# A hybrid decoder step on one core: one buffer for inner features after the first step, and four reordered pieces of side work

## The chip, the core and the metric

The kernel runs on one core of a Trainium2 chip. Its time is the device time of one execution in microseconds, given as the median of the runs. TensorE (PE) does the matmuls, VectorE (DVE), ScalarE (ACT) and GpSimd (POOL) do the elementwise work, and SyncE (SP) issues the transfers. Each engine works off its own queue in program order: an instruction that waits holds up all that stand behind it on its engine.

## What is computed

One layer of inference on 1024 prompt tokens and 8 x 8 decode tokens (1088 in all), width 1024, in float32. The output is compared with this reference, cut here to what matters:

```python
h = rmsnorm(x, g_mix_pre) * (1 + scale_m) + shift_m
sc_b, sc_c, sc_x, z, xbc, dt = split(h @ w_in)
y_sc = sc_b * causal_dwconv(sc_c * sc_x, sc_conv_w)        # also returns the new conv state
y_ssd = ssd_scan(silu(causal_dwconv(xbc)), dt, ...)        # 16 heads, 4 groups
y_ssd = rmsnorm((y_ssd * silu(z)) per group) * ssm_norm_g  # four norms, one for each group
x = x + gate_m * rmsnorm(concat(y_sc, y_ssd) @ w_out, g_mix_post)
h2 = rmsnorm(x, g_ffn_pre) * (1 + scale_f) + shift_f
x = x + gate_f * rmsnorm((silu(h2 @ w_gate) * (h2 @ w_up)) @ w_down, g_ffn_post)
```

## The kernel before, in words

Every float32 operand of a large matmul is split into two parts, hi (a cast, done by ScalarE, line 1039 or 311) and lo (the difference, done by VectorE, line 1040 or 312), and each product is three matmuls: hi by hi, hi by lo, lo by hi. So a weight tile that arrives by DMA costs a cast on ScalarE and a subtraction on VectorE before PE can use it, and the third matmul of a chain needs the lo part. The function `part` does one such split.

From the short-convolution columns on, and in the FFN, blocks are multiplied with seven products instead of eight (`unit`). Products are taken in the order 1, 5, 6, 3, 7, 2, 4; the sums of weight blocks that some of them need are made by `combos_w`, those of the features by `sums_h`, `sums_last` and `sums_x`. `plain_w` splits four weight blocks without sums.

The stretches that matter here, in order of time:

1. The gates z of groups 2 and 3 (`gate_late`), with the steps of the generator `sums` in between. Group 3's weights are split by `plain_w`, called at line 1186, behind gate 2.
2. Four pairs of column tiles of the short convolution. Each pair runs three units, cc, cx and cb (`sc_unit`), then the convolution. Beside the units of the first pair the norms of groups 2 and 3 (`norm`) are taken in steps: sums of squares, an rsqrt chain of small VectorE operations on a tile sm, a broadcast on PE (line 291), multiplications (line 939), the split into hi and lo (lines 298 and 299) and the store of both halves to y_d in DRAM (`y_out`). The tiles y of pair 1 take the memory of group 3's.
3. The output projection in phases. The first takes the SSD half, eight column tiles in four pairs mp, and calls `conv_state`, which transposes the new conv state (8 transposes, 2 copies, 2 stores). Then `out_proj` adds the other half for three ranges of tokens, and runs a generator `tail` (`mix_tail`) of the tokens whose sum is complete: transposes and squares of the first four column tiles; the same of the last four, then rsqrt, residual (line 1260) and its squares; a second rsqrt and a scaling; transposes back.
4. The FFN. `plain_step(j, q)` does block j of the inner width for token half q with plain products: four gate blocks (evacuated by ScalarE into sg), four up blocks (multiplied by VectorE into f), and `inner_out`, which writes f and sums of it into f_d in DRAM through tiles fs. Those come in turn from the pools in the list `st_from`. Steps (0,0) and (1,0) come first, while `tail` generators finish the tokens of the second half; then the memory `tailp` is closed, a new pool `xc1a` is laid out where it was, `plain_x` makes x__1224 to x__1227 in it, and step (0,1) begins with them.

What sets the order: the program is written in one order, a scheduler with priorities puts it into engine queues, and work that is wrapped in `in_order` or `chained` may not pass the last PE instruction before it. Pools of memory add waits: a tile waits for the last reader of what its memory held before. The list `st_from` at the FFN's start:

```python
    st_from.append(pool(tailp, "stx", 1))
    plain_step(0, 0, ...)
    ...
    plain_step(1, 0, ...)
    run(tail_a, tail_b)
    st_from.pop(st_from.index(next(p for p in st_from if p is not st0)))
    tailp.close()
```

Of the kernel before, what the change touches and what calls it, by code (L numbers as in the profile page):

```python
# [33 lines left out]
def hymba_step(ctx, tc, i, o):  # L34
# [927 lines left out]
    def run(*gens):  # L962
        for gen in gens:
            for _ in gen:
                pass
# [100 lines left out]
    def plain_w(w, cols, raws=None):  # L1066
        raws = raws or [raw_half(w, j, cols) for j in range(2)]
        W = {}
        for m in range(2):
            for j in range(2):  # L1070
                t = in_turn(w_from).tile([P, 2, 4, P], F32R, tag="wc", name=nm("wp_"))
                part(t[:, 0], t[:, 1], raws[j][:, :, m * P:(m + 1) * P])
                W[m, j] = [[t[:, s, k] for k in range(4)] for s in range(2)]
        return W

# [105 lines left out]
        return psy.tile([P, 2, 384], F32, tag="sq", name=nm("sq"))  # L1181

    sums = sums_h()
    norm2, norm3 = (norm(g, ys[g], sq_row, sx_row) for g in (2, 3))
    gate_late(2, ys[2], [[v[:, k] for v in w for k in range(KT)] for w in w_next], {n: [sums] for n in range(6)})
    W = plain_w(w_in, 3072 + 768, raw_next[:2])
    gate_late(3, ys[3], [[W[m, j][s][k] for s in range(2) for j in range(2) for k in range(4)] for m in range(2)],
              {n: [sums] for n in range(6)})
    run(sums)
# [3 lines left out]
    def sc_unit(cols, tiles, between):  # L1193
        unit(combos_w(w_in, cols, nc.vector), X_sc, 4, [0, 1],
             lambda q, i, h: tiles[i][:, SQ[q][0] + 272 * h:SQ[q][0] + 272 * (h + 1)], True, between, SQ, chained)

    kept = []
    for pr in range(4):
        cc, cx = [yt((pap, yp2)[pr % 2]) for _ in range(2)], [yt(yp4) for _ in range(2)]
        sc_unit(1024 + 256 * pr, cc, {})  # L1200
        sc_unit(2048 + 256 * pr, cx, {n: [norm2, norm2] for n in range(7)} if pr == 0 else {})
        if pr == 0:
            run(norm2)
        if pr == 2:
            conv_state(ncs, 16, 3, o["ssmc_p"], o["ssmc_s"])
        ext = []
        for m in range(2):
            ct = 2 * pr + m
            e = yt(yp4, (P, YT))
            es = e[:, 2 + NP:2 + NP + 80].rearrange("p (b t) -> p b t", b=8)  # L1210
            nc.vector.tensor_tensor(e[:, 2:2 + NP], cc[m][:, :NP], cx[m][:, :NP], op=mult)
            nc.vector.tensor_tensor(es[:, :, 2:10], bt(cc[m][:, NP:]), bt(cx[m][:, NP:]), op=mult)
            keep_tail(e, es, hscT[:, ct, :], nsc[:, ct, :], 2)
            conv(cc[m], e, es, [scw[:, j, ct:ct + 1] for j in range(3)], ct, None)
            ext.append(e)
        cb = [yt(yp4) for _ in range(2)]
        sc_unit(256 * pr, cb, {n: [norm3, norm3] for n in range(7)} if pr == 0 else {})
        if pr == 0:
            run(norm3)
        for m in range(2):  # L1220
            y, hi, lo = cc[m], ext[m][:, :T].bitcast(F32R), cb[m].bitcast(F32R)
            nc.vector.tensor_tensor(y, y, cb[m], op=mult)
            split(hi, lo, y)
            kept.append((2 * pr + m, hi, lo))
        if pr < 3:
            while kept:
                y_out(*kept.pop(0))
# [62 lines left out]
    for mp in range(4):  # L1290
        for m, (wh, wl) in enumerate(load_cols(w_out, mp * 256, 2, D)):
            for c0, n in OC:
                ps = pm()
                acc3(ps, n, [(wh[:, k, :], wl[:, k, :], first[k][0][:, c0:c0 + n], first[k][1][:, c0:c0 + n])
                             for k in range(KT)])
                nc.scalar.copy(acc_at(2 * mp + m, c0, n), ps[:, :n])
        if mp == 0:
            while kept:
                y_out(*kept.pop(0))
        if mp == 2:  # L1300
            conv_state(nsc, 8, 2, o["scc_p"], o["scc_s"])


    def out_split(c):
# [22 lines left out]
    def out_proj(c, terms, steps_, load, pairs=range(4)):  # L1327

        for mp in pairs:
            for m, w in enumerate(load(mp)):  # L1330
                m += 2 * mp
                in_order(out_tile, c, terms, w, m)
                for gen in steps_.get(m, ()):
                    in_order(next, gen, None)
# [52 lines left out]
    nxt = next_splits()  # L1387
    out_proj(0, terms[0], {0: [nxt], 2: [nxt]}, out_load)
    tail = mix_tail([0, 1, 2, 3], lambda t: load_x(t, fb, "fm"), rows_fm, G_m)
    out_proj(1, terms[1], {0: [tail], 1: [tail], 4: [tail]}, out_load)  # L1390
    out_proj(2, terms[2], {1: [tail], 2: [tail]}, out_load, (0, 1))


# [64 lines left out]
    def mark():  # L1458
        while True:
            marks.append(in_line())  # L1460
            yield
# [117 lines left out]
    tail_b = mix_tail([6, 7, 8], x_tl, row_tl, G2)  # L1579
    st_from.append(pool(tailp, "stx", 1))  # L1580
    plain_step(0, 0, ({0: [tail_b], 2: [tail_b], 3: [tail_a]}, {0: [tail_a], 1: [tail_a, mark()], 3: [tail_b]}))
    raw_from = [btp] * 4
    w_from = [slots[1]] * 4 + [slots[0]] * 4
    g0 = sums_x([xc0], 0)
    s0 = behind(g0)
    plain_step(1, 0, ({0: [tail_b], 1: [tail_b]}, {1: [s0], 2: [s0], 3: [s0]}))
    run(tail_a, tail_b)
    st_from.pop(st_from.index(next(p for p in st_from if p is not st0)))
    tailp.close()
    xc1 = [pool(left, "xc1a", 1)]  # L1590
    run(plain_x(xc1[0], 1))
# [176 lines left out]
```

## Time and profile before

| | |
|---|---|
| median of 3 runs | 1768.85 us (1767.85 to 1770.19) |
| profiled execution | 1771.54 us, its span 1769.8 us |
| mean granted clock of PE | 0.983 |
| PE busy | 1695.9 us, 96% of the span |
| DVE busy | 1170.4 us, 66% |
| ACT busy | 777.2 us, 44% |
| POOL busy | 210.8 us, 12% |

A share of the span is an average over stages. PE's queue is what ends last nearly everywhere, so the table is read together with PE's own waits: where PE stands idle, the timeline names the instruction that released it. [...]

### The profile page before, as it was taken

Reading aid. Unit: us, or ns where it says so; the run is one execution under the profiler, and the core shown is the slowest. Engines: PE = TensorE matmul, PEld = TensorE weight load, DVE = VectorE, ACT = ScalarE, POOL = GpSimd, SP = SyncE. Lnnn points to the kernel's source line nnn. Section 1 sums busy time; section 2 is a strip of 40 time slices with the busy share of each in tenths; the row PEclk is TensorE's granted clock in tenths of the full one; section 3 lists DMA queues with packets and bytes.
Section 4 is the critical chain, followed back from the end, with each engine's and each line's share of the span. In section 5 each row is a group of like instructions: output and inputs, shape, how many; then the busy total and the mean of one; then the engine's idle time right before and its main releaser. Section 6 shows DMA issues by size and latency. Waiting matters only on the chain.

```text
span 1769.8 us, 31580 instructions
## 1 busy us (share of the span) xinstructions
PE 1695.9 (96%) x12628; PEld 1608.7 (91%) x12628; DVE 1170.4 (66%) x2264; ACT 777.2 (44%) x1601; POOL 210.8 (12%) x317
## 2 busy tenths in 40 slices
PE   5999999999999999999999979999999999899997
PEld 4898888898899999998989979999999999899987
DVE  5578677777888676551137769666665676677845
ACT  3447454557444333322227755444444454422303
POOL 2110000000000000000000000122222200322303
PEclk9999999999999999999999989999999999999999
DMA  9201345442222422258275542334344349756243
GB/s 317 69 18 32 112 148 158 139 124 76 102 72 99 149 87 65 99 207 278 74 242 190 181 155 88 114 137 164 139 149 149 137 146 336 299 213 237 99 152 120
DMA packets 160634, 259.74 MB, mean 147 GB/s; under 512 B 10561, under 2 KB 124401, under 8 KB 158182
## 3 DMA queue, kind: packets, MB, share of 16 engines
q1 hardware_dynamic: 160486, 257.71, 42.8%
q8 instruction: 99, 1.62, 0.4%
q14 instruction: 49, 0.40, 0.1%
HBM read 186.30 MB, written 71.38 MB: 146 GB/s over the span
## 4 chain that ended last, share of the span: by engine, by line
PE 81%; DVE 8%; ACT 4%; DMA 3%; issue 2%; POOL 1%; SPq 1%; DVEq 0%; ACTq 0%; POOLq 0%
PE pm L334 10%; PE pm L336 10%; PE pm L335 9%; PE pz L1078 7%; PE pz L1080 7%; PE pz L1079 7%; PE pm L1080 6%; PE pm L1078 6%; PE pm L1079 6%; DMA raw<-in_w_in 1%; PE pm L209 1%; PE pz L751 1%; PE pz L756 1%; PE pz L745 1%; PE pz L723 1%
## 5 line engine op out<-in xcount | busy, mean ns | idle before, releaser
L312 DVE TENSOR_TENSOR wl<-raw,wh 128x512 fp32r<-128x512 f32 (+1 forms) x87 | 61.4, 730 | 99.9 <-ACT wh L311 99.2
L334 PE MATMUL pm<-h,wh 128*128 128x384 f32 (+1 forms) x342 | 114.8, 336 | 0.0
L335 PE MATMUL pm<-h,wh 128*128 128x384 f32 (+1 forms) x342 | 114.5, 335 | 0.0
L336 PE MATMUL pm<-h,wl 128*128 128x384 f32 (+1 forms) x342 | 113.7, 334 | 0.0
L336 PE MATMUL pm<-hb,wl 128*128 128x512 f32 (+2 forms) x320 | 107.5, 337 | 1.9 <-DVE wl L312 1.9
L335 PE MATMUL pm<-hb,wh 128*128 128x512 f32 (+2 forms) x320 | 107.4, 337 | 0.0
L334 PE MATMUL pm<-hb,wh 128*128 128x512 f32 (+2 forms) x320 | 105.4, 336 | 1.3 <-ACT wh L311 1.3
L311 ACT CAST wh<-raw 128x512 fp32r<-128x512 f32 (+1 forms) x89 | 56.4, 664 | 113.5 <-PE pm L335 70.0
L1040 DVE TENSOR_TENSOR fs<-f,fs 128x576 fp32r<-128x576 f32 (+2 forms) x80 | 56.0, 713 | 28.2 <-ACT fs L1039 27.3
L1039 ACT CAST fs<-f 128x576 fp32r<-128x576 f32 (+2 forms) x80 | 46.6, 597 | 51.3 <-DMA f_d<-fs 22.1
L336 PEld LDWEIGHTS pm<-hb,wl 128*128 128x128 f32 x320 | 60.7, 190 | 7.4 <-DVE wl L312 2.1
L1095 DVE TENSOR_TENSOR facc<-facc,pz 128x288 f32<-128x288 f32 x124 | 55.9, 451 | 16.9 <-PE pz L1080 16.5
L334 PEld LDWEIGHTS pm<-hb,wh 128*128 128x128 f32 x320 | 60.5, 190 | 7.1 <-ACT wh L311 1.6
L334 PEld LDWEIGHTS pm<-h,wh 128*128 128x128 f32 x342 | 65.2, 191 | 1.6 <-issue 0.9
L335 PEld LDWEIGHTS pm<-h,wh 128*128 128x128 f32 x342 | 65.2, 191 | 1.4 <-issue 0.7
L336 PEld LDWEIGHTS pm<-h,wl 128*128 128x128 f32 x342 | 64.9, 190 | 1.3 <-issue 1.0
L335 PEld LDWEIGHTS pm<-hb,wh 128*128 128x128 f32 x320 | 60.7, 190 | 5.1
L1095 DVE TENSOR_TENSOR facc<-facc,pm 128x256 f32<-128x256 f32 x124 | 51.5, 415 | 6.5 <-PE pm L1080 5.6
L334 PE MATMUL pm<-bt,wh 128*128 128x384 f32 (+2 forms) x146 | 51.6, 353 | 0.0
L336 PE MATMUL pm<-bt,wl 128*128 128x384 f32 (+1 forms) x146 | 48.5, 332 | 0.2 <-DVE wl L312 0.2
L1057 POOL TENSOR_TENSOR raw<-raw 128x512 f32<-128x512 f32 x16 | 22.6, 1412 | 217.0 <-DVE raw L1055 208.4
L335 PE MATMUL pm<-bt,wh 128*128 128x384 f32 (+2 forms) x146 | 47.7, 327 | 0.0
(7510 smaller groups left out, 6390.0 us busy)
## 6 DMA issues: line engine op xcount, KB each, us to landing
raw<-in_w_in SPq DMA_DIRECT2D x48, 512.0 KB
fc<-f_d SPq DMA_DIRECT2D x9, 2016.0 KB
f_d<-fs SPq DMA_DIRECT2D x31, 576.0 KB
wa<-in_w_ada SPq DMA_DIRECT2D x32, 512.0 KB
raw<-in_w_out SPq DMA_DIRECT2D x32, 512.0 KB
fc<-f_d SPq DMA_DIRECT2D x9, 1792.0 KB
f_d<-fs SPq DMA_DIRECT2D x31, 512.0 KB
raw<-in_w_gate SPq DMA_DIRECT2D x28, 512.0 KB
```

The source lines that it names most:

```text
L311: (nc.gpsimd.tensor_copy if hi_eng else nc.scalar.copy)(wh, raw)
L312: (eng or nc.vector).tensor_tensor(wl, raw, wh, op=sub)
L334: mm(ps[:, :n], wh, xh, start=(first and j == 0), stop=False)
L335: mm(ps[:, :n], wh, xl, start=False, stop=False)
L336: mm(ps[:, :n], wl, xh, start=False, stop=(last and j == end))
L1039: nc.scalar.copy(hi, v)
L1040: (eng or nc.vector).tensor_tensor(lo, v, hi, op=sub)
L1057: eng.tensor_tensor(a21, a11, a21, op=sub)
L1078: mm(ps, W[0][k], X[0][k], start=(start and k == 0), stop=False, skip_group_check=True)
L1079: mm(ps, W[0][k], X[1][k], start=False, stop=False, skip_group_check=True)
L1080: mm(ps, W[1][k], X[0][k], start=False, stop=(stop and k == nk - 1), skip_group_check=True)
L1095: nc.vector.tensor_tensor(out(q, i, h), out(q, i, h), ps, op=add)
```

## The change

Five edits, none of which adds or removes an instruction on any engine:

- the split of gate 3's weights is written ahead of gate 2;
- the norms of groups 2 and 3 become one generator `norms`, stepped once in the last four products of cc, once in each product of cx and twice in each of cb, without the calls that ran them to their ends;
- `conv_state` for the short convolution runs in order, behind the third pair of the first phase;
- the steps of `tail` in the second phase stand behind column tiles 0, 2 and 5 instead of 0, 1 and 4;
- after step (0,0), `st_from` holds st0 alone, so that step (1,0) writes all its fs tiles through one buffer and none through stx, which lies in `tailp`.

```diff
--- before.py
+++ after.py
@@ -1181,9 +1181,9 @@
         return psy.tile([P, 2, 384], F32, tag="sq", name=nm("sq"))
 
     sums = sums_h()
-    norm2, norm3 = (norm(g, ys[g], sq_row, sx_row) for g in (2, 3))
+    norms = itertools.chain(*(norm(g, ys[g], sq_row, sx_row) for g in (2, 3)))
+    W = plain_w(w_in, 3072 + 768, raw_next[:2])
     gate_late(2, ys[2], [[v[:, k] for v in w for k in range(KT)] for w in w_next], {n: [sums] for n in range(6)})
-    W = plain_w(w_in, 3072 + 768, raw_next[:2])
     gate_late(3, ys[3], [[W[m, j][s][k] for s in range(2) for j in range(2) for k in range(4)] for m in range(2)],
               {n: [sums] for n in range(6)})
     run(sums)
@@ -1197,10 +1197,8 @@
     kept = []
     for pr in range(4):
         cc, cx = [yt((pap, yp2)[pr % 2]) for _ in range(2)], [yt(yp4) for _ in range(2)]
-        sc_unit(1024 + 256 * pr, cc, {})
-        sc_unit(2048 + 256 * pr, cx, {n: [norm2, norm2] for n in range(7)} if pr == 0 else {})
-        if pr == 0:
-            run(norm2)
+        sc_unit(1024 + 256 * pr, cc, {n: [norms] for n in range(3, 7)})
+        sc_unit(2048 + 256 * pr, cx, {n: [norms] for n in range(7)})
         if pr == 2:
             conv_state(ncs, 16, 3, o["ssmc_p"], o["ssmc_s"])
         ext = []
@@ -1214,9 +1212,7 @@
             conv(cc[m], e, es, [scw[:, j, ct:ct + 1] for j in range(3)], ct, None)
             ext.append(e)
         cb = [yt(yp4) for _ in range(2)]
-        sc_unit(256 * pr, cb, {n: [norm3, norm3] for n in range(7)} if pr == 0 else {})
-        if pr == 0:
-            run(norm3)
+        sc_unit(256 * pr, cb, {n: [norms, norms] for n in range(7)})
         for m in range(2):
             y, hi, lo = cc[m], ext[m][:, :T].bitcast(F32R), cb[m].bitcast(F32R)
             nc.vector.tensor_tensor(y, y, cb[m], op=mult)
@@ -1298,7 +1294,7 @@
             while kept:
                 y_out(*kept.pop(0))
         if mp == 2:
-            conv_state(nsc, 8, 2, o["scc_p"], o["scc_s"])
+            in_order(conv_state, nsc, 8, 2, o["scc_p"], o["scc_s"])
 
 
     def out_split(c):
@@ -1387,7 +1383,7 @@
     nxt = next_splits()
     out_proj(0, terms[0], {0: [nxt], 2: [nxt]}, out_load)
     tail = mix_tail([0, 1, 2, 3], lambda t: load_x(t, fb, "fm"), rows_fm, G_m)
-    out_proj(1, terms[1], {0: [tail], 1: [tail], 4: [tail]}, out_load)
+    out_proj(1, terms[1], {0: [tail], 2: [tail], 5: [tail]}, out_load)
     out_proj(2, terms[2], {1: [tail], 2: [tail]}, out_load, (0, 1))
 
 
@@ -1579,13 +1575,13 @@
     tail_b = mix_tail([6, 7, 8], x_tl, row_tl, G2)
     st_from.append(pool(tailp, "stx", 1))
     plain_step(0, 0, ({0: [tail_b], 2: [tail_b], 3: [tail_a]}, {0: [tail_a], 1: [tail_a, mark()], 3: [tail_b]}))
+    st_from[:] = [st0]
     raw_from = [btp] * 4
     w_from = [slots[1]] * 4 + [slots[0]] * 4
     g0 = sums_x([xc0], 0)
     s0 = behind(g0)
     plain_step(1, 0, ({0: [tail_b], 1: [tail_b]}, {1: [s0], 2: [s0], 3: [s0]}))
     run(tail_a, tail_b)
-    st_from.pop(st_from.index(next(p for p in st_from if p is not st0)))
     tailp.close()
     xc1 = [pool(left, "xc1a", 1)]
     run(plain_x(xc1[0], 1))
```

In ScalarE's queue, around the first casts of the second token half. fs is a tile on its way to f_d, sg a gate block, x__1224 to x__1227 the features, wp__ and w__ weights. Before:

```order
832 L1039 CAST x__1218_10780<-acc_8212 128x1024
833 L1039 CAST fs_10810<-f_10502 128x512
834 L1039 CAST fs_10826<-f_10502 128x512
835 L1039 CAST fs_10820<-f_10502 128x512
836 L1039 CAST x__1224_10836<-acc_8208 128x1152
837 L1039 CAST x__1225_10839<-acc_8208 128x1152
838 L1039 CAST x__1226_10842<-acc_8208 128x1152
839 L1039 CAST x__1227_10845<-acc_8208 128x1152
840 L1518 ACTIVATE sg_10848<-pz_10866 128x288
```

After:

```order
822 L1514 ACTIVATE sg_10501<-pm_10628 128x256
823 L1039 CAST x__1224_10836<-acc_8208 128x1152
824 L1039 CAST x__1225_10839<-acc_8208 128x1152
825 L1039 CAST x__1226_10842<-acc_8208 128x1152
826 L1514 ACTIVATE sg_10501<-pm_10654 128x256
827 L1039 CAST x__1227_10845<-acc_8208 128x1152
828 L1039 CAST wp__1234_10860<-raw_10850 128x512
829 L1039 CAST wp__1235_10863<-raw_10852 128x512
```

The four x casts stood behind three fs casts; now they stand 13 places up, between the evacuations of step (1,0)'s gate, and the fs casts come after them, the first at row 836.

In VectorE's queue at gate 3: wp__ are gate 3's weights, x__63n sums of features for the units. Before:

```order
683 L1040 TENSOR_TENSOR x__633_4859<-y_4964,x__633_4859 128x544
684 L910 TENSOR_TENSOR y_2515<-y_2515,pm_5001 128x320
685 L1040 TENSOR_TENSOR x__637_4863<-y_4965,x__637_4863 128x544
686 L1040 TENSOR_TENSOR wp__653_5031<-raw_4717,wp__653_5031 128x512
687 L1150 TENSOR_TENSOR y_4965<-y_4965 128x2x272
688 L1040 TENSOR_TENSOR wp__654_5034<-raw_4719,wp__654_5034 128x512
689 L1040 TENSOR_TENSOR wp__655_5037<-raw_4717,wp__655_5037 128x512
690 L1040 TENSOR_TENSOR x__641_4867<-y_4965,x__641_4867 128x544
691 L1040 TENSOR_TENSOR wp__656_5040<-raw_4719,wp__656_5040 128x512
```

After:

```order
671 L1147 TENSOR_TENSOR y_4883<-y_4883,y_4882 128x2x272
672 L1040 TENSOR_TENSOR wp__631_4831<-raw_4717,wp__631_4831 128x512
673 L1040 TENSOR_TENSOR wp__632_4834<-raw_4719,wp__632_4834 128x512
674 L1040 TENSOR_TENSOR wp__633_4837<-raw_4717,wp__633_4837 128x512
675 L1040 TENSOR_TENSOR wp__634_4840<-raw_4719,wp__634_4840 128x512
676 L1040 TENSOR_TENSOR x__636_4870<-y_4882,x__636_4870 128x544
677 L1040 TENSOR_TENSOR x__640_4874<-y_4883,x__640_4874 128x544
```

The four lo parts of gate 3's weights come some 14 places sooner, before the first sums of features.

In VectorE's queue in the second phase of the output projection: the operations on x with sm are the residual step of `tail`, wl_9531 belongs to column tile 5, wl_9610 to tile 6. Before:

```order
1129 L285 SCALAR_TENSOR_TENSOR sm_9427<-sm_9427 128x4
1130 L1260 SCALAR_TENSOR_TENSOR x_9330<-y_9338,sm_9427,x_9330 128x1024
1131 L1260 SCALAR_TENSOR_TENSOR x_9332<-y_9339,sm_9427,x_9332 128x1024
1132 L1260 SCALAR_TENSOR_TENSOR x_9334<-y_9340,sm_9427,x_9334 128x1024
1133 L1260 SCALAR_TENSOR_TENSOR x_9336<-y_9341,sm_9427,x_9336 128x1024
1134 L1325 TENSOR_TENSOR acc_8208<-acc_8208,pm_9494 128x304
1135 L312 TENSOR_TENSOR wl_9531<-raw_9520,wh_9530 128x512
1136 L312 TENSOR_TENSOR wl_9531<-raw_9522,wh_9530 128x512
1137 L1325 TENSOR_TENSOR acc_8208<-acc_8208,pm_9536 128x304
1138 L279 TENSOR_SCALAR sm_9562<-ssn 128x4
```

After, from the last rsqrt operation on:

```order
1132 L285 SCALAR_TENSOR_TENSOR sm_9469<-sm_9469 128x4
1133 L1256 SCALAR_TENSOR_TENSOR x_9330<-y_9338,sm_9469,x_9330 128x1024
1134 L1256 SCALAR_TENSOR_TENSOR x_9332<-y_9339,sm_9469,x_9332 128x1024
1135 L1256 SCALAR_TENSOR_TENSOR x_9334<-y_9340,sm_9469,x_9334 128x1024
1136 L1256 SCALAR_TENSOR_TENSOR x_9336<-y_9341,sm_9469,x_9336 128x1024
1137 L1321 TENSOR_TENSOR acc_8208<-acc_8208,pm_9536 128x304
1138 L1321 TENSOR_TENSOR acc_8208<-acc_8208,pm_9562 128x304
1139 L312 TENSOR_TENSOR wl_9610<-raw_9605,wh_9609 128x512
1140 L312 TENSOR_TENSOR wl_9610<-raw_9607,wh_9609 128x512
1141 L279 TENSOR_SCALAR sm_9588<-ssn 128x4
```

Before, the weights of tile 5 stood behind the four residual operations. After, they stand ahead (rows 1125 and 1127), and those of tile 6 stand behind.

## Rows read from the trace of the kernel before

**Rows 1.** The page: busy time and share of TensorE; the chain that ended last, by engine.
```profile
PE 1695.9 (96%) x12628; PEld 1608.7 (91%) x12628; DVE 1170.4 (66%) x2264; ACT 777.2 (44%) x1601; POOL 210.8 (12%) x317
PE 81%; DVE 8%; ACT 4%; DMA 3%; issue 2%; POOL 1%; SPq 1%; DVEq 0%; ACTq 0%; POOLq 0%
```
**Rows 2.** Timeline of PE, second token half of the FFN: start, us, engine, line, operation [idle before <-releaser].
```profile
1054.30 0.61 PE L334 MATMUL pz<-x__1224_10836,wp__1232_10854 128*128 128x288 f32 x1 [9.20 <-ACT x__1224_10836 L1039]
1055.69 0.61 PE L335 MATMUL pz<-x__1224_10836,wp__1232_10854 128*128 128x288 f32 x1 [0.79 <-DVE x__1224_10836 L1040]
...
1088.04 0.30 PE L1078 MATMUL pz<-x__1227_10845,w__1267_11172 128*128 128x288 f32 x1
```
**Rows 3.** Timeline of PE, gate 3 and the first short-convolution unit.
```profile
484.18 0.69 PE L336 MATMUL pm<-bt,wp__653_5031 128*128 128x384 f32 x1 [3.21 <-DVE wp__653_5031 L1040]
...
510.54 0.29 PE L1078 MATMUL pm<-bt,w__677_5263 128*128 128x272 f32 x1
...
525.12 0.39 PE L1078 MATMUL pm<-h,w__683_5285 128*128 128x272 f32 x1 [1.28 <-ACT h L1039]
...
525.88 0.39 PE L1079 MATMUL pm<-h,w__683_5285 128*128 128x272 f32 x1 [0.37 <-DVE h L1040]
```
**Rows 4.** Timeline of PE, ScalarE and SyncE (SPq) around the first two pairs.
```profile
580.26 2.27 PE L291 MATMUL pz<-ident,sm 128*128 128x128 f32 x18 [1.35 <-DVE sm L285]
...
595.11 0.32 SPq L950 DMA_DIRECT2D y_d<-y  x1
...
598.32 0.39 ACT L1093 COPY y<-pm 128x272 f32<-128x272 f32 x1 [0.69 <-DMA y_d<-y]
...
598.76 0.39 PE L1078 MATMUL pm<-h,w__755_6103 128*128 128x272 f32 x1 [2.07 <-ACT y L1093]
```
**Rows 5.** Timeline of PE, first phase of the output projection.
```profile
809.30 0.50 PE L334 MATMUL pm<-hb,wh 128*128 128x512 f32 x1 [1.28 <-ACT wh L311]
```
**Rows 6.** Timeline of VectorE and PE, second phase of the output projection.
```profile
940.69 4.87 DVE L1260 SCALAR_TENSOR_TENSOR x<-y,sm,x 128x1024 f32<-128x1024 f32 x4
...
946.60 0.41 PE L336 MATMUL pm<-hb,wl 128*128 128x304 f32 x1 [1.90 <-DVE wl L312]
```
**Rows 7.** Windows of PE: stretch, us, busy (instructions), granted clock, DMA share, GB/s.
```profile
484.00:490.20 6.20, 6.02 (x19) 0.51 0.50 148
598.70:603.40 4.70, 4.64 (x25) 0.64 0.29 115
937.60:941.00 3.40, 3.40 (x27) 1.00 0.27 92
946.60:950.60 4.00, 4.00 (x19) 0.61 1.02 329
1054.30:1060.80 6.50, 5.71 (x24) 0.55 0.32 129
```
**Rows 8.** Timeline of GpSimd, SyncE, ScalarE and VectorE around the casts of x__1224.
```profile
1027.98 2.52 POOL L1372 TENSOR_TENSOR acc<-acc,modT 128x64 f32<-128x64 f32 x8 [24.56 <-DVE acc L1371]
...
1049.72 0.34 SPq L1543 DMA_DIRECT2D f_d<-fs  x1
...
1051.50 0.62 ACT L1039 CAST fs<-f 128x512 fp32r<-128x512 f32 x1 [3.42 <-issue]
...
1053.10 1.15 ACT L1039 CAST x__1224_10836<-acc 128x1152 fp32r<-128x1152 f32 x1
...
1054.28 1.36 DVE L1040 TENSOR_TENSOR x__1224_10836<-acc,x__1224_10836 128x1152 fp32r<-128x1152 f32 x1 [0.36 <-ACT x__1224_10836 L1039]
...
1084.66 0.68 DVE L1040 TENSOR_TENSOR w__1267_11172<-raw,w__1267_11172 128x512 fp32r<-128x512 f32 x1
```
**Rows 9.** Windows of VectorE, columns as in rows 7.
```profile
475.00:500.00 25.00, 23.86 (x35) 0.86 0.28 86
...
1049.00:1062.40 13.40, 8.94 (x12) 0.62 0.43 157
1062.40:1085.40 23.00, 20.40 (x25) 1.00 0.00 1
```

## The prediction

> **What bounds the kernel now.** I read the page first: TensorE (PE) is busy 96% of the span and carries 81% of the chain that ended last [rows 1]. The change leaves the number of instructions on every engine as it is, so only the 74 us in which PE stands still, and the slow matmuls behind those waits, can be won or lost. The next view is the timeline of PE: the waits that lie where the change moves something are 9.20 and 0.79 us before the first gate matmuls on the second token half [rows 2], 3.21, 1.28 and 0.37 us around gate 3 [rows 3], 1.35 and 2.07 us in the first pairs of the short convolution [rows 4], 1.28 us in the first phase of the output projection [rows 5] and 1.90 us in its second [rows 6]. The third view is the granted clock by stretch [rows 7]. [...] The loss is busy time by the missing share: 6.02 x 0.49 = 3.0 us after the 3.21 wait, 4.64 x 0.36 = 1.7 after the 2.07 wait, 4.00 x 0.39 = 1.6 after the 1.90 wait, 5.71 x 0.45 = 2.6 after the 9.20 wait. Behind the waits of 1.28 and 1.35 us no slow stretch shows in the timeline, so I charge none for waits up to 1.4 us and 1.7 for those near 2.
>
> **Part A, st_from back to one buffer after the first step.** Before: ScalarE casts x__1224 at 1053.10, behind three fs casts of step (1,0), one of them after 3.42 us of waiting [rows 8]. The data for x__1224 is ready when GpSimd ends at 1027.98 + 2.52 = 1030.5 [rows 8], 23 us sooner. The tile sits in the memory of the pool that also holds stx, so it could not start until the stores from stx had left. After: the order shows the four x casts 13 places up, ahead of every fs cast of that step. Four casts at 1.15 us start at 1031 and end at 1035.7; VectorE (DVE), idle there, does its four halves at 1.36 us [rows 8] by about 1037.4. PE comes at 1045.1, so the wait of 9.20 + 0.79 goes, and the slow stretch of 2.6 with it: 12.6 us.
>
> What is late next: PE now reaches the third product of the next unit (w__1267) not at 1088.04 [rows 2] but 12.6 us sooner, at about 1075.5. DVE had that weight split at 1084.66 + 0.68 = 1085.3 [rows 8], after 23.0 us in which it was busy for 20.4 [rows 9]. In the new order 36 operations of DVE stand between its free moment at 1049.0 and the end of w__1267; by the rows of the old trace they take 26.7 us, so it can't be ready before 1075.7. Replaying the queues of ScalarE and DVE row by row with old durations, and with 1.78 us from the issue of a store to the next cast in its buffer (1049.72 to 1051.50 [rows 8]), I get 1078.0. That is a new wait of 2.5 us, in two pieces of 1.2 and 1.3 (hi half, then lo half), so without a clock charge. Part A: -12.6 + 2.5 = -10.1. Bounds: -12.6 (no wait) to 0 (DVE as late as before, 9.8 us of wait).
>
> The same edit leaves three fs casts each waiting for the store before it, in ScalarE's queue, with gate evacuations, weight casts and x casts behind them. In the replay they stand at 1053.6, 1057.1 and 1061.1; the cast after the last of them waits for DVE until 1064.2 anyway. So 3 us of slack cover two store times, and the cost is zero while a store takes under 3.2 us.
>
> **Part B, gate 3's split ahead of gate 2.** DVE is busy 23.9 of 25 us here [rows 9]. The four lo operations move from rows 686 to 691 of its queue to rows 672 to 675, and are done at 476.4, where PE wants them at 484.18 - 3.21 = 481.0. The wait of 3.21 and its 3.0 of slow clock go, and PE gets to the short convolution at 504.3 instead of 510.54 [rows 3]. But DVE has the same work to do, and the later operations shift: my replay has the weights of the second product at 508.5, where PE comes at 507.4, those of the third at 514.1 where PE comes at 511.5, and the last input half 0.3 us late. So 1.1 + 2.6 + 0.3 = 4.0 us are given back; the old waits of 1.28 and 0.37 are in that. The wait of 2.6 is nearest to the rows of 1.90 and 2.07: 1.7 of clock. Part B: -(3.21 + 3.0 + 1.28 + 0.37) + 4.0 + 1.7 = -2.2. Bounds: -7.9 and 0.
>
> **Part C, norms in one generator, taken from the first unit on.** Same instructions. Norm 3's broadcast still waits for DVE's rsqrt chain, 0.85 us instead of 1.35. More counts at the end: the copy into y waits for DMA y_d<-y, whose last store was issued at 595.11, and PE behind it 2.07 us [rows 4]. In the new order the store of norm 3's second half stands ahead of the two convolution stores and of one weight load in SyncE's queue; I have it issued about 3.5 us after the unit before ends, against 8 before, and landed 3 us ahead of need. Wait and slow stretch go: 2.07 + 1.7. The first weights of pair 1 are now split behind norm 3's multiplications in DVE's queue, with 4 us to spare. Part C: -0.5 - 3.8 = -4.3. Bounds: -5.2 (the wait of 1.35 gone whole) and -0.5 (the store is late as before).
>
> **Part D, conv_state held in order.** Its eight transposes and two copies stood right ahead of weights that PE then missed by 1.28 us [rows 5]. Without them PE arrives about as much sooner as the weight cast does, so a wait stays, and the transposes cost the same later. Its two stores now stand behind copies that ScalarE does at about 858, ahead of two weight loads that are used 20 us later: covered; if that cover were gone, SyncE would hold those loads for one store. Part D: -0.1. Bounds: -1.3 and +1.
>
> **Part E, a tail step two tiles later.** Before: DVE applies the residual in one block of 4.87 us [rows 6]; the weights of tile 5 stand behind it, and PE waits 1.90. After: the order has the weights of tile 5 ahead of the block, but those of tile 6 behind it. The block moves with its step by one tile (3.4 us [rows 7]) and starts at 944.2, not 940.69; with two evacuations behind it and the first half of the split, tile 6 has its weights at 950.55, and PE wants them at 948.05. The wait is 2.5 instead of 1.90, with 1.7 of clock again: part E is +0.6 to +0.7. I take +0.6. Bounds: -3.5 (the block fits) and +2.
>
> **Sum**: -10.1 - 2.2 - 4.3 - 0.1 + 0.6 = -16.1. The profiled execution took 1771.54 us, 1.7 more than its span and 2.7 more than the median of the runs, 1768.85. It gives 1755.4 for a profiled execution; on the median, 1752.7, and I say 1753.
>
> [...] The rows show a slow stretch after 1.90 and none after 1.35. [...]
>
> **Rivals.** (1) The new waits are smaller than in my replay: DVE and ScalarE find gaps that I filled, the block of part E fits, and no clock is lost. A -10.1, B -3.9, C -4.3, E -3.5, D -0.1: -21.9, 1747. For it: DVE has gaps around 1049 to 1062 [rows 9]. Against: it is nearly full in B. (2) DVE sets the pace, and each piece won is given back there: w__1267 comes at 1085, and the units of B at their old times. A 0, B 0, C -0.5 to -4.3: 1764.5 to 1768.5. If besides every new wait carries a slow stretch (A +2.6, B +1.7, E +2 with C at -0.5), it is 1774: slower. The point of decision is whether w__1267 is split more than 7 us after my 1078. Against: x__1224 to x__1227 leave that stretch of its queue, and what stood before them was waiting, not work. (3) The change doesn't do what it says in A: x__1224 still waits for something in the freed memory. Only B to E remain: -6.0, 1763. Against: the order puts it ahead, and its named waits are for ScalarE's and GpSimd's own earlier results. (4) Slow stores on the one buffer: each microsecond over 3.2 us in two stores delays w__1267 twice. The longest comparable row, 595.11 to the copy at 598.32 [rows 4], is 3.2: it costs nothing, and 1753 stays.
>
> **How the numbers follow.** Forecast 0.52; rival 1 0.22; rival 2 0.12, of which slower 0.05 and within the bound 0.07; rival 3 0.06; 0.08 for what I haven't seen (0.05 faster, 0.02 same, 0.01 slower). 0.2%, about what a measurement of this kernel can tell from no change, is 3.5 us. Faster: 0.52 + 0.22 + 0.06 + 0.05 = 0.85; same 0.09; slower 0.06. The bounds of the parts, taken as independent, reach about 8 us to either side of 1753; the range goes to 1743 below, past rival 1, and to 1764 above, past rival 3. It leaves out rival 2 and a share of what is unseen.
>
> **What would show it.** Right: no PE wait before x__1224, one of 2 to 3 us before w__1267 some 14 us further; no wait at wp__ in gate 3, and new ones at w__679 and w__680; none on y_d<-y; a wait of 2 to 3 us on wl in the second output projection, one tile later, with PE's clock low after it. Wrong: PE waits of over 5 us on DVE lo halves between the first gate step on the second half and the unit behind it, or ScalarE waiting for f_d<-fs for more than 3 us at a time.

## The result and the profile after

The changed kernel takes 1749.03 us, the median of 4 runs (1748.26 to 1749.48), against 1769.52 for the kernel before (4 runs beside it, 1767.85 to 1773.56): a ratio of 0.988, 95% interval 0.9863 to 0.9898, or 20.5 us less. The forecast was 1753, with a range of 1743 to 1764.

Two rows of the page of after answer to [rows 1]: the busy times, and the chain that ended last.

```profile
PE 1688.8 (97%) x12628; PEld 1603.8 (92%) x12628; DVE 1166.8 (67%) x2264; ACT 777.9 (45%) x1601; POOL 213.7 (12%) x317
...
PE 33%; DVE 4%; ACT 2%; POOL 1%; DMA 1%; issue 1%; SPq 0%; DVEq 0%; POOLq 0%; ACTq 0%
```

The counts of instructions are those of before. PE's busy time fell by 7.1 us with the same matmuls, while its mean granted clock went from 0.983 to 0.987 over the span (1695.9 x 0.004 / 0.987 = 6.9 us, an estimate from these two figures); the other 15.2 us between the two spans are standing still that is gone. The chain's shares add up to 42% only (it could be followed back no further), so they are not set against the 81% of [rows 1].

Where the time went is read by following one and the same instruction through both traces. Here are PE's timeline of after (start, us, engine, line, operation, the wait ahead of it in brackets), and then the rows of before that [rows 2 to 6] don't hold.

```profile
502.34 0.29 PE L1078 MATMUL pm<-bt,w__677_5263 128*128 128x272 f32 x1
...
509.56 0.39 PE L1078 MATMUL pm<-x__640_4874,w__680_5275 128*128 128x272 f32 x1 [0.99 <-ACT w__680_5275 L1039]
...
511.10 0.39 PE L1080 MATMUL pm<-x__640_4874,w__680_5275 128*128 128x272 f32 x1 [1.02 <-DVE w__680_5275 L1040]
...
521.81 0.29 PE L1078 MATMUL pm<-h,w__681_5278 128*128 128x272 f32 x1
...
591.34 0.29 PE L1078 MATMUL pm<-bt,w__756_6106 128*128 128x272 f32 x1
...
796.09 0.50 PE L334 MATMUL pm<-hb,wh 128*128 128x512 f32 x1 [0.99 <-ACT wh L311]
...
938.08 0.41 PE L336 MATMUL pm<-hb,wl 128*128 128x304 f32 x1 [2.12 <-DVE wl L312]
...
975.35 0.36 PE L334 MATMUL pm<-x__1114_9935,wp__1141_10106 128*128 128x256 f32 x1
...
994.99 0.66 PE L1356 MATMUL pz<-ident,x 128*128 128x128 f32 x4 [2.10 <-ACT x L1348]
...
1009.83 0.28 PE L334 MATMUL pm<-x__1130_10005,wp__1192_10510 128*128 128x256 f32 x1
...
1034.13 0.30 PE L334 MATMUL pz<-x__1224_10836,wp__1232_10854 128*128 128x288 f32 x1
...
1065.89 0.40 PE L1080 MATMUL pz<-x__1227_10845,w__1267_11172 128*128 128x288 f32 x1 [0.75 <-DVE w__1267_11172 L1040]
...
1084.28 0.28 PE L1078 MATMUL pm<-x__1114_9935,w__1292_11423 128*128 128x256 f32 x1
```

```profile
527.75 0.29 PE L1078 MATMUL pm<-h,w__681_5278 128*128 128x272 f32 x1
...
603.39 0.29 PE L1078 MATMUL pm<-bt,w__756_6106 128*128 128x272 f32 x1
...
987.76 0.36 PE L334 MATMUL pm<-x__1114_9935,wp__1141_10106 128*128 128x256 f32 x1
...
1006.65 0.66 PE L1360 MATMUL pz<-ident,x 128*128 128x128 f32 x4 [1.65 <-ACT x L1352]
...
1020.65 0.28 PE L334 MATMUL pm<-x__1130_10005,wp__1192_10510 128*128 128x256 f32 x1
...
1106.84 0.28 PE L1078 MATMUL pm<-x__1114_9935,w__1292_11423 128*128 128x256 f32 x1
```

The execution profiled after is 2.0 us ahead at 64 us already, in the opening that the change doesn't touch; that is how two executions differ, and is taken off:

| up to the start of | before | after | less 2.0 | share of this stretch |
|---|---|---|---|---|
| w__681 (behind gate 3 and the first unit) | 527.75 | 521.81 | 3.9 | B -3.9 |
| w__756 (second pair) | 603.39 | 591.34 | 10.1 | C -6.1 |
| wp__1141 (FFN) | 987.76 | 975.35 | 10.4 | D and E -0.4 |
| wp__1192 (step (1,0)) | 1020.65 | 1009.83 | 8.8 | not foreseen: +1.6 |
| w__1292 | 1106.84 | 1084.28 | 20.6 | A -11.7 |

From w__1292 the two traces run in parallel to the end: 22.3 us between the spans, 20.3 less the 2.0. The waits of 9.20 and 0.79 us before x__1224 [rows 2], of 3.21, 1.28 and 0.37 [rows 3], of 1.35 and 2.07 [rows 4] are gone. New are 0.99 and 1.02 us at w__680 and 0.75 at w__1267; the wait behind the residual block has moved by one tile and is 2.12 instead of 1.90 [rows 6]. The transposes of x at 994.99 wait 2.10 us, 1.65 before; no term of the sum was about them.

### The profile page after: what moved, and what is told of

The parts are those of the page before. It is cut to its first block, busy times and chain, and to the rows that moved or that the text cites. A ratio compares the mean times of both kernels' runs of the same rounds, so it can differ in the third digit from the quotient of the medians.

```text
span 1747.5 us, 31578 instructions
## 1 busy us (share of the span) xinstructions
PE 1688.8 (97%) x12628; PEld 1603.8 (92%) x12628; DVE 1166.8 (67%) x2264; ACT 777.9 (45%) x1601; POOL 213.7 (12%) x317
```

## The experiments

The spread between executions was up to 12 us for one and the same kernel, so the times settle signs and sizes of some us; the local readings come from the traces, in which the waits named here came back to a few hundredths.

### One part alone

**A alone** is the kernel before with

```diff
     plain_step(0, 0, ...)
+    st_from[:] = [st0]
...
-    st_from.pop(st_from.index(next(p for p in st_from if p is not st0)))
```

> The kernel before with one edit: st_from is set back to [st0] after step (0,0). Theory (the parts add up, each as the trace of after shows it): -11.5 us, 1758.0; the waits of 9.20 and 0.79 us before x__1224 gone, and about 0.75 us of wait at w__1267. By the figure of the prediction: -10.1, 1759.4, with 2.5 us of wait at w__1267; the smaller wait of after would then be owed to the other parts. Rival (VectorE sets the pace in that stretch): 0 to -3.

Measured: 1758.07 us, ratio 0.9934 (0.9917 to 0.995). Rows of PE's timeline of this kernel, to [rows 2] and the table:

```profile
1007.69 0.66 PE L1360 MATMUL pz<-ident,x 128*128 128x128 f32 x4 [2.10 <-ACT x L1352]
...
1046.87 0.30 PE L334 MATMUL pz<-x__1224_10836,wp__1232_10854 128*128 128x288 f32 x1
...
1078.63 0.40 PE L1080 MATMUL pz<-x__1227_10845,w__1267_11172 128*128 128x288 f32 x1 [0.75 <-DVE w__1267_11172 L1040]
```

The wait at w__1267 is 0.75 without B to E as well, so 2.5 was wrong by itself. Up to wp__1141 (987.79) this trace runs with that of before to 0.05 us. Then the wait at the transposes is 2.10 here too, and with the slow stretch behind it (granted clock 0.74 from 1007.6 to 1014.2, where before has 1.00 from 1006.6 to 1013) wp__1192 is 1.9 us later than before. From there A wins 11.8; net it is 9.9 us at w__1292. By this run alone the unforeseen +1.6 of the table could be A's; the runs below don't bear that out.

**All but A** is the kernel after without its line `st_from[:] = [st0]`, and with the removal of the second buffer back in its old place:

```diff
-    st_from[:] = [st0]
...
     run(tail_a, tail_b)
+    st_from.pop(st_from.index(next(p for p in st_from if p is not st0)))
```

> The kernel after without part A (two buffers for fs until the tail's memory closes, as before). Theory: parts B to E alone, -3.9 - 6.1 - 0.4 + 1.6 = -8.8 us, 1760.7; the waits of 9.20 and 0.79 us stand before x__1224 as in the kernel before, 9 us sooner. By the figures of the prediction: -6.0, 1763.5. If A's gain leans on B to E, the sum of this run and of A alone differs from the whole -20.5 by more than 1 us.

Measured: 1756.19 us, ratio 0.9934 (0.9915 to 0.9953). The waits of 9.19 and 0.78 us stand before x__1224 as they did [rows 2], and the transposes wait 2.11. By the trace w__1292 is 15.2 us sooner than before, 12.7 less the 2.5 that it was ahead at the start of the short convolution (w__677) beyond B's 6.2. A's 9.9 and these 12.7 make 22.6, 2.0 more than the whole at that place. That difference is worked out from three sizes: this execution has no slow stretch behind w__680 (1.5 us) nor behind the residual block (granted clock 1.00 there, 0.58 in after: about 1.7), while the loss at the transposes (1.6) is in both parts and counts once in the whole. 1.5 + 1.7 - 1.6 = 1.6 of the 2.0. So by the traces, and by a working made after the fact, the parts add up to 0.4 us. The times can't tell: by the medians the two runs win 13.0 and 14.8 us, 27.8 together against 20.5, but each of the two has an interval of about 3 us to either side.

D and E were not run alone. **B alone** and **C alone** are the kernel before with one piece of the diff each (of C's, behind its first two lines, only the new lines are shown):

```diff
+    W = plain_w(w_in, 3072 + 768, raw_next[:2])
     gate_late(2, ys[2], ...)
-    W = plain_w(w_in, 3072 + 768, raw_next[:2])
```

```diff
-    norm2, norm3 = (norm(g, ys[g], sq_row, sx_row) for g in (2, 3))
+    norms = itertools.chain(*(norm(g, ys[g], sq_row, sx_row) for g in (2, 3)))
...
+        sc_unit(1024 + 256 * pr, cc, {n: [norms] for n in range(3, 7)})
+        sc_unit(2048 + 256 * pr, cx, {n: [norms] for n in range(7)})
...
+        sc_unit(256 * pr, cb, {n: [norms, norms] for n in range(7)})
```

> The kernel before with gate 3's split written ahead of gate 2, nothing else. Theory: -3.9 us, 1765.6; the wait of 3.21 us in gate 3 gone, about 1 us each before w__680's hi and lo halves, no wait before the last input half. By the prediction: -2.2, 1767.3, with 1.1, 2.6 and 0.3 us of wait. Rival (VectorE, full in this stretch, gives all back): 0, 1769.5.

> The kernel before with the norms in one generator, taken from the first unit of the short convolution on; nothing else. Theory: -6.1 us, 1763.4; no wait of 1.35 us at norm 3's broadcast and none of 2.07 us before the units that read y. By the prediction: -4.3, 1765.2, with 0.85 us left at the broadcast. Rival (the wait at the broadcast went only since B shifts VectorE's queue): the wait of 1.35 us stays here, and the gain is 3.8 to 4.3.

B measured 1765.59 us, ratio 0.9968 (0.9957 to 0.998); C 1763.98, ratio 0.9956 (0.994 to 0.9972). In B alone w__680 waits 0.99 and 1.02 as in after, w__681 comes 5.5 us sooner than before, not 3.9, and the last input half waits 0.24. The difference is the clock, in PE's windows over w__680's waits (stretch, us, busy, granted clock, DMA share, GB/s), of after, of after a second time, of B alone and of all but A:

```profile
509.50:515.50 6.00, 4.92 (x25) 0.72 0.33 94
```

```profile
506.60:512.60 6.00, 4.89 (x24) 0.72 0.30 92
```

```profile
511.30:515.70 4.40, 3.36 (x24) 1.00 0.10 16
```

```profile
509.00:513.50 4.50, 3.40 (x25) 1.00 0.13 18
```

From w__680 to w__682 it is 5.9 us in the first two and 4.4 in the others. In C alone, the wait at the broadcast is gone without B, so the rival falls; between w__681 and w__756 it wins 6.5 us. About 1 us of that is a step of the norms that stands ahead of w__681 in this run (in before and after it stands behind). Ahead of w__681 it also meets a slow stretch that before hasn't, behind the same waits of 1.28 and 0.37 us; PE's windows there, of before and of C alone:

```profile
521.00:527.00 6.00, 4.35 (x33) 1.00 0.00 0
```

```profile
521.00:527.00 6.00, 4.35 (x24) 0.80 0.00 0
```

The clock differs at gate 3 too: the old wait of 3.20 us in gate 3 is there, but the granted clock behind it is 0.76 where before had 0.51 [rows 7], and w__677 comes 1.5 us sooner. PE's window:

```profile
484.00:490.20 6.20, 6.08 (x27) 0.76 0.49 150
```

### After, a second time, and one use of the second buffer

The second run of after has no edit. The other one sends the second of the four fs tiles of step (1,0) through stx again (the pool of the list that is not st0):

```diff
-    st_from[:] = [st0]
...
+    st_from[:] = [st0, next(p for p in st_from if p is not st0), st0, st0]
     plain_step(1, 0, ...)
+    st_from[:] = [st0]
```

> The kernel after a second time, unchanged. What depends on the order of the instructions should return to a few hundredths of a microsecond: 0.99 and 1.02 us of wait at w__680, 2.12 at the weights of tile 6 of the second output projection, 0.75 at w__1267. Theory: the slow stretch behind w__680 (1.5 us in the first profile, none in the two kernels with the same two waits and B but not A and C together) and the load of w_up that lands 7.3 us after its issue (5.8 in before) are chance, so the stretch may be missing and the wait of 2.10 before the transposes of x may be 1.65. Rival: both belong to the order of the instructions, and return. Time: -20.5 us against before, by up to 3 either way.

> The kernel after, but the second of the four fs tiles of step (1,0) goes through stx again. Theory: what counts for x__1224 is when the last tile that uses the tail's memory has left; the second tile's cast is the first to run, so ScalarE gets to x__1224 at about 1029 instead of 1020, 5 us ahead of need: no wait, the time of after within 0.5 us. Rival (the second buffer as such makes the wait, through the order of the casts): x__1224 is late by some microseconds of the old 9.20. Second rival: with any use of stx the whole wait of 9.2 + 0.8 us returns, +10 to +12 us.

After again: 1746.71 us (1740.55 to 1752.85), ratio 0.9871 (0.9847 to 0.9895). The waits named return to 0.01 us: 0.99 and 1.02, 2.12, 0.75, and 2.11 at the transposes; so does the slow stretch behind w__680, and the chance that I gave both came out against me here. The other profiles say more of the transposes. In before the load of w_up is issued at 986.41 and cast at 992.21, 5.8 us later; in A alone it is issued at 986.43 and cast at 994.03, 7.6 us later, and ScalarE and the transposes come late with it. Here are SyncE's issue and ScalarE's cast in the kernel without A, and the same with PE's transposes in the kernel with A and two residual rows on GpSimd (below):

```profile
970.45 1.12 SPq L1035 DMA_DIRECT2D raw<-in_w_up  x2
...
977.76 0.62 ACT L1039 CAST wp__1210_10684<-raw 128x512 fp32r<-128x512 f32 x1 [2.42 <-DMA raw<-in_w_up]
```

```profile
973.57 1.12 SPq L1035 DMA_DIRECT2D raw<-in_w_up  x2
...
979.72 0.62 ACT L1039 CAST wp__1210_10686<-raw 128x512 fp32r<-128x512 f32 x1 [1.26 <-DMA raw<-in_w_up]
...
993.81 0.66 PE L1356 MATMUL pz<-ident,x 128*128 128x128 f32 x4 [1.65 <-ACT x L1348]
```

Where the load takes 5.8 to 6.4 us from issue to cast (before, B alone, C alone, two rows on GpSimd), the transposes wait 1.65; where it takes 7.1 to 8.7 (after twice, A alone, all but A, one use of stx), they wait 2.10 or 2.11. Both groups have kernels with A and without. So the loss goes with the load and is not shown to be A's. Why the load takes longer no row shows; this stays open.

With one use of stx the profiled execution took 1752.31 us, 7.0 more than the profiled one of after again (1745.34). ScalarE's part of my theory held, VectorE's did not. Rows of ScalarE and VectorE of this kernel, then PE's:

```profile
1027.85 1.15 ACT L1039 CAST x__1225_10839<-acc 128x1152 fp32r<-128x1152 f32 x1
1028.90 1.15 ACT L1039 CAST x__1226_10842<-acc 128x1152 fp32r<-128x1152 f32 x1
```

```profile
1036.26 1.35 DVE L1040 TENSOR_TENSOR x__1225_10839<-acc,x__1225_10839 128x1152 fp32r<-128x1152 f32 x1
...
1038.80 1.35 DVE L1040 TENSOR_TENSOR x__1226_10842<-acc,x__1226_10842 128x1152 fp32r<-128x1152 f32 x1
```

```profile
1040.21 0.61 PE L335 MATMUL pz<-x__1226_10842,wp__1233_10857 128*128 128x288 f32 x1 [7.46 <-DVE x__1226_10842 L1040]
```

ScalarE has the hi half of x__1226 at 1030, in time, but the lo half stands 10 us further on in VectorE's queue, behind the sums of the acc blocks, the differences on f and the fs tiles; in after the four lo halves run one behind the other from 1021.38 to 1026.6. So A's gain hangs on the place of the casts on both engines, and a single use of the tail's memory puts enough of that off to lose 7.46 of the 9.99 us again. A second buffer outside the tail's memory would have told memory and buffer count fully apart; it wasn't tried.

### The waits that are left

Three places were tried: the residual block (E), the transposes of x, and the two together.

**Two of the four residual rows on GpSimd**:

```diff
-    def mix_tail(ts, x_new, row_new, G):
+    def mix_tail(ts, x_new, row_new, G, on_pool=()):
...
-        yield from residual_rows(..., keep)
+        yield from residual_rows(..., keep, pool=on_pool)
...
-    tail = mix_tail([0, 1, 2, 3], ..., G_m)
+    tail = mix_tail([0, 1, 2, 3], ..., G_m, (1, 3))
```

> The kernel after with two of the four residual rows of the tail in the second output projection taken from VectorE: ScalarE scales them and GpSimd adds. Theory: VectorE's block of 4.88 us is what the weights of tile 6 stand behind; halved to 2.44 it ends 2.4 us sooner, the wait of 2.12 goes, and with it the slow stretch of 1.7: -2.1 to -3.8 us against after. Rival: GpSimd's adds slow VectorE's operations beside them, or the scaling on ScalarE holds up the next casts, and a wait of 1 to 2 us stays.

Measured: 1749.61 us, ratio 0.9891 (0.987 to 0.9912). Rows of the timelines of VectorE, GpSimd and PE in this kernel:

```profile
927.15 4.73 DVE L1256 SCALAR_TENSOR_TENSOR x<-y,sm,x 128x1024 f32<-128x1024 f32 x2
```

```profile
928.38 5.71 POOL L1254 TENSOR_TENSOR x<-x,y 128x1024 f32<-128x1024 f32 x2 [179.54 <-ACT y L1253]
```

```profile
935.84 0.62 PE L334 MATMUL pm<-hb,wh 128*128 128x304 f32 x1 [4.80 <-ACT wh L311]
```

Two rows take VectorE 4.73 us here. In after four take 4.88 with nothing on GpSimd beside them, 1.28 each, with 1.20 from one start to the next. So of the 4.73 some 1.2 are the first row's, nearly all ahead of GpSimd's start at 928.38, and 3.53 the second's, beside GpSimd's first add of 2.42 us and the start of its second: 2.25 more than a row alone, nearly as much as that add. And ScalarE's squares wait 0.45 and 1.06 us for GpSimd, the weights stand behind them, and PE waits 4.80 us.

**The rsqrt of tail_a ahead of tail_b's residual**, and **tail_a's transposes one block later**:

```diff
-    plain_step(0, 0, ({0: [tail_b], 2: [tail_b], 3: [tail_a]}, {0: [tail_a], 1: [tail_a, mark()], 3: [tail_b]}))
+    plain_step(0, 0, ({0: [tail_b], 2: [tail_a], 3: [tail_b]}, {0: [tail_a], 1: [tail_a, mark()], 3: [tail_b]}))
```

```diff
-    plain_step(0, 0, ({0: [tail_b], 2: [tail_b], 3: [tail_a]}, {0: [tail_a], 1: [tail_a, mark()], 3: [tail_b]}))
+    plain_step(0, 0, ({0: [tail_b], 2: [tail_b], 3: [tail_a]}, {1: [tail_a, mark()], 2: [tail_a], 3: [tail_b]}))
```

> The kernel after with the third step of tail_a (rsqrt and scaling of x) one block earlier and the second step of tail_b (its residual) one block later in the gate unit of step (0,0). Theory: the wait of 2.10 and 0.38 us before the transposes of x is owed to two rsqrt chains that run interleaved behind the residual sums of tail_b on ScalarE and VectorE; with tail_a's chain first both waits go, and the slow stretch of 1.6 us behind them: -2.5 to -4.1 us against after. Rival (the load of w_up, which lands late, sets it): the wait moves to the next weights, and the time is after's within 1 us. Rival: tail_b's residual, one block later, holds up VectorE ahead of the products of the up unit: 0 to +3.

> The kernel after with the fourth and fifth step of tail_a (transposes of the scaled rows and their evacuation) one block later in the up unit of step (0,0). Theory: ScalarE ends the scaling of x 1.0 us after TensorE wants it at the earliest and TensorE waits 2.10 and 0.38 us; one block is some 3.5 us, so both waits go, and nothing behind them is due sooner than the next unit: -2.5 to -4.1 us against after. Rival: the weights wp__1191 of the next unit, cast on ScalarE behind the evacuations that now come later, are late by 1 to 4 us (0.50 us of wait on VectorE there already): -1 to +2.

The first: 1748.64 us, ratio 0.9887 (0.9865 to 0.9909). The wait of 2.10 is gone, but 0.99 us comes at the same transposes and 1.88 and 0.38 at those of tail_b, 15 us on. The second: 1749.35, ratio 0.9883 (0.9868 to 0.9898), and the wait is 2.96 at wp__1191. Both times the wait moved on, as rivals had it: in the second to the weights named, in the first to tail_b's transposes and not to weights. ScalarE is busy for 21.69 of the 28.00 us from 984 to 1012 in after, VectorE for 19.51, and what was put first there delayed what stands behind it, in these two runs by the waits named.

**The residual in halves**, the second half behind tile 6 and the scaling step behind tile 7 (mid, the last argument of mix_tail, names the row behind which a step ends):

```diff
                 done(t, tn, res[tt], cols)
+            if tt in mid:
+                yield
...
-    tail = mix_tail([0, 1, 2, 3], ..., G_m)
+    tail = mix_tail([0, 1, 2, 3], ..., G_m, (1,))
-    out_proj(1, terms[1], {0: [tail], 2: [tail], 5: [tail]}, out_load)
-    out_proj(2, terms[2], {1: [tail], 2: [tail]}, out_load, (0, 1))
+    out_proj(1, terms[1], {0: [tail], 2: [tail], 6: [tail], 7: [tail]}, out_load)
+    out_proj(2, terms[2], {2: [tail], 3: [tail]}, out_load, (0, 1))
```

> The kernel after with the residual of the tail in the second output projection in two halves of two rows: the second half is taken behind tile 6 instead of in one piece with the first, the scaling step behind tile 7, the two transposing steps one tile later each. Theory: VectorE's block of 4.88 us is the whole cause of the wait of 2.12 us; in halves of 2.44, with the weights of tile 6 between them, TensorE doesn't wait: -2.1 us against after, and -3.8 where the slow stretch goes too. Rival: ScalarE's scaling ends too late for the transposes, with a wait of 1 to 3 us there: 0 to +1.

Measured: 1746.1 us, ratio 0.987 (0.9853 to 0.9886). No wait is left at the weights, and PE's window there is full and fast:

```profile
934.00:942.00 8.00, 8.00 (x60) 1.00 0.89 326
```

From w__756 to wp__1141 this takes 380.7 us, against 384.0 in both profiles of after, and 382.4 in all but A, which has the wait of 2.13 but a whole clock behind it: 3.3 us are won, 1.7 of them without the clock, and the block was the cause. Behind it the transposes wait 2.43 and 1.11 us appears at tail_b's, so that in time it is not told from after.

**Both edits**, and then **tail_b's last three steps one block later besides**, so that the next unit's weights stand ahead of its scaling on ScalarE:

```diff
-    plain_step(0, 0, ({0: [tail_b], 2: [tail_b], 3: [tail_a]}, {1: [tail_a, mark()], 2: [tail_a], 3: [tail_b]}))
+    plain_step(0, 0, ({0: [tail_b], 2: [tail_b], 3: [tail_a]}, {1: [tail_a, mark()], 2: [tail_a]}))
...
-    plain_step(1, 0, ({0: [tail_b], 1: [tail_b]}, {1: [s0], 2: [s0], 3: [s0]}))
+    plain_step(1, 0, ({0: [tail_b], 1: [tail_b], 2: [tail_b]}, {1: [s0], 2: [s0], 3: [s0]}))
```

> The two edits (transposes of tail_a one block later, residual in halves) together. Theory: the two places lie 50 us apart and share nothing that is late, so the sum: -4.6 to -7.9 us against after, about 1742 where after has 1747 to 1749. Rival: what one gains the next wait takes: -1 to +1.

> The kernel with both edits (residual in halves, transposes of tail_a one block later) and besides tail_b's last three steps one block later, so that the casts of the next unit's weights (wp__1191 and its neighbours) stand ahead of tail_b's scaling on ScalarE. Theory: the wait of 2.65 us at those weights comes from ScalarE's queue, in which 3.23 us of scaling stand ahead of them; with that order turned the wait goes, the transposes of tail_b have a block more, and x__1224 is still cast in the same place of the queue: the 3.3 us of the residual and the 2.5 to 4.1 us of the transposes are kept, 5 to 7 us below after, about 1742. Rival: the transposes of tail_b or x__1224 are late instead, by 1 to 3 us: within 2 us of the kernel with the two edits alone, 1748.

The two edits alone: 1747.96 us, ratio 0.9876 (0.9861 to 0.9891), with 2.65 us of wait at wp__1191. With the third: 1742.05 us (1738.06 to 1746.56), ratio 0.9836 (0.9809 to 0.9863), the fastest of all. ScalarE's rows of the kernel with two edits, and of that with three:

```profile
999.63 3.24 ACT L1350 ACTIVATE x<-x,sm 128x1024 f32<-128x1024 f32 x3
1002.75 0.63 ACT L1039 CAST fs<-f 128x512 fp32r<-128x512 f32 x1
1003.26 0.64 ACT L1039 CAST wp__1191_10507<-raw 128x512 fp32r<-128x512 f32 x1
```

```profile
1000.55 0.63 ACT L1039 CAST wp__1191_10494<-raw 128x512 fp32r<-128x512 f32 x1
1001.07 0.63 ACT L1039 CAST wp__1192_10497<-raw 128x512 fp32r<-128x512 f32 x1
1001.74 0.62 ACT L1039 CAST wp__1193_10500<-raw 128x512 fp32r<-128x512 f32 x1
1002.26 1.15 ACT L1350 ACTIVATE x<-x,sm 128x1024 f32<-128x1024 f32 x1
```

The weights' casts now come first, no wait over 0.3 us is left between 800 and 1059, and PE's clock is whole over the old slow stretch:

```profile
986.00:1000.00 14.00, 13.76 (x110) 1.00 0.59 189
```

From w__756 to w__1292 it takes 486.1 us; after has 492.9 and 494.0 in its two profiles. So 6.9 to 7.9 us are won at the place, at the upper end of the 5 to 7 expected and a little past it.

## Why the prediction was right, and where it was not

**What held.** The direction, and the mechanism of each part: PE finds x__1224 ready, w__1267 is the next thing late, the waits move from gate 3 to the first short-convolution unit, the wait on y_d<-y goes, the residual block's wait moves by one tile with its clock. 1749.0 lies between the forecast of 1753 and rival 1's 1747, nearer to the rival's. The sum came 4.4 us short (-16.1 for -20.5): it had 1.6 too little in A, 1.7 in B, 1.8 in C and 0.9 in D and E, and lacked the loss of 1.6 at the transposes, which hid part of that.

**A: term 2.5 for w__1267 was too large.** It was 0.75 in after, after again and A alone, and also in the last kernel of the experiments, where no wait lies ahead of it that could hide a longer one. My replay had the split end at 1078.0 with 26.7 us of work behind 1049.0, that is 2.3 us of gaps. In after VectorE has nearly none in this stretch (window as above, VectorE):

```profile
1036.00:1066.70 30.70, 29.98 (x42) 1.00 0.31 114
```

So the lower bound of that step, the pure sum of work, was nearer than the replay. That VectorE is full here is rival 2's picture; its price didn't come, since the x halves had left the stretch. Stores on the one buffer held ScalarE for 2.70 us once (1050.53), and nothing behind it was late: rival 4 as told. By itself A wins 11.7 to 11.8 us, for the 10.1 that were said. The transposes of x ahead of it lost 1.6 to 1.9 us, a term that the sum didn't have; the runs tie it to the load of w_up and not to A. That A alone came out at -9.9 is these two errors cancelling, which is luck.

**B: term 4.0 of new waits was too large.** 0.99 + 1.02 = 2.0 came, nothing at w__679 (1.1 was said), and the last input half waits 0.24 (0.3 was said) only where the clock is not slow ahead of it. The clock's 1.7 was near: 1.5 in after. So -3.9 for -2.2, and -5.5 in B alone without the slow stretch.

**C: term 0.85 for norm 3's broadcast was wrong.** No wait is left there, with B and without it; -6.1 for -4.3, past the bound of -5.2 by 0.9; 0.4 of that is a wait that no term named, 0.91 us on w__726 in before and 0.49 on w__729 in after. The 3.8 for the y_d<-y wait and its clock are within that sum, and were right in kind: the wait is gone.

**D and E: +0.5 was said, -0.4 came.** The wait was 2.12 for 2.5, at the tile named, with the granted clock at 0.58 over 938 to 942. At 796.09 the weights still wait 0.99, so D's charge of next to nothing stands.

**The charges for the clock.** The forecast without the 3.4 us charged for two new slow stretches would have been 1749.3 (1752.7 less 3.4), which is near what came; but not for that reason: both stretches are in after's profile (granted clock 0.72 behind w__680's waits, 0.58 behind the residual block's), and in that of after a second time (0.72 and 0.61). That such a stretch can stay away behind the same wait is shown by other profiles, told in the last section. The errors of the parts are in the main that every new wait of the replay was longer than the real one.

## What to carry to other kernels

A replay of the queues with old durations finds the right next wait, but overstates it; set its result beside the plain sum of work on the engine that is late, and where that engine is nearly full, lean to the sum. When a wait goes, look also at the smaller waits near it that the change leaves alone: here the next ones were two tails on ScalarE, and moving one step only passed the wait on, until the cast that someone waits for stood ahead of the scaling that no one does. Give memory that a later stage needs no new tenant in the step before it: one tile was enough to put off the splits of the next stage, for which PE then waited 7.46 us.

## What the runs showed of the hardware

Most waits of one order repeat to 0.01 us between executions (0.99, 1.02, 2.12 and 0.75 in both profiles of after); not all do: before the transposes of acc at 983.77 PE waits 0.89 us in the second profile of after, and not in the first. The clock behind the waits repeats less. Behind w__680's 0.99 and 1.02 us there is a slow stretch of about 1.5 us in 8 of 11 profiles and none in 3; in ten of the eleven, two of those three among them, nothing is edited against after up to there. Behind the residual block's wait of 1.90 to 2.13 the granted clock was 0.57 to 0.65 in nine profiles and 1.00 in one. Behind 1.65 us at the transposes it was 1.00 in two kernels and 0.73 in two; before the second pair it was 0.64 in before (behind 2.07 us) and in A alone, and 1.00 in B alone. Behind 1.28 and 0.37 us in the first unit it was 1.00 in before and A alone, and fell in C alone (0.80 from 521 to 527). So in these profiles a slow stretch was a chance, not a charge, and the length of the wait didn't settle it; my line between 1.4 and 2 us was too sharp.

Two more things were not expected: a VectorE row beside a GpSimd add of 2.42 us took 3.53 us instead of 1.28, and one and the same load took 5.8 us from issue to cast in one profile and up to 8.7 in another, which is open.
